# mLSTM layer of a fp32r decoder step: value projection with tokens stationary, gate columns beside the first head's values, shuffle for the sample's row pairs, and the first heads' order

## The chip, the cores and the metric

The kernel runs on one core of a Trainium2 chip. The metric is device microseconds of one execution, as the median of three runs. TensorE is called PE, VectorE DVE, ScalarE ACT, GpSimd POOL and the queue that issues the transfers SP, as the profile does.

## What is computed

One inference step of a two-layer decoder trunk on 320 tokens: one prompt of 256 and a sample group of 8 sequences with 8 tokens each. Layer 0 mixes tokens by a spatial gating MLP, layer 1 by an mLSTM matrix memory, and behind each mixer stands a gated feed-forward layer with a short convolution. The change lies in layer 1's mixer, and there in how `v` and the gates `i`, `f` are projected:

```python
p = x @ w_in                                   # x: tokens x 1024, already normed
qk_pre = p[..., :QK_B]                         # 2048 columns: 8 heads of q, 8 of k
v      = p[..., QK_B:QK_B + D_B]               # 2048 columns: 8 heads x 256
o_pre  = p[..., QK_B + D_B:QK_B + 2 * D_B]     # 2048 columns
i_pre, f_pre = the last 16 columns             # 8 input gates, 8 forget gates
...
ig = i_pre + b_i;  lf = log_sigmoid(f_pre + b_f)
h, C, n, m = mlstm_chunkwise(q, k, v, ig, lf, C0, n0, m0)   # all gates of a head from cumulated lf
```

## The kernel before, in words

Activations lie transposed (features on partitions, 320 token columns). Every fp32 operand is split in a high and a low fp32r half, and a product is three matmuls: high by high, high by low, low by high. A weight tile of 128 x 1024 numbers is brought by SP (`prefetch`, 4 raw buffers), then split by ACT (`wh`, the cast, L167) and DVE (`wl`, the difference, L168) one block ahead of its use (3 buffers of halves). `block` then issues 24 matmuls (8 slices of the features, three products) with a 128 x 128 weight slice stationary and the 320 tokens moving, into one PSUM bank of the pool `psm` (3 banks); all else takes its banks from `psa` (5).

Layer 1's mixer, `layer_b`, goes head by head (h = 0 to 7). A head's six blocks are q, k, two of v and two of o. Its steps by name:

- `gates` (L729): the gates' block `pg`, whose weights hold each gate column twice (16 matmuls); the norm's column sums, `norm_cols`, `norm_row` and `norm_twice`; then head 0's q, k, v, v, o, o and head 1's q, and between them on DVE and ACT the chain that makes the gates: a log-sigmoid (L777 to L781, with two loads of ACT tables), two scans (L782, L787), and exponentials into `Xf` and `RS`. `Xf` is spread over the partitions by a matmul into `pMb`, `RS` is turned to columns by transposes into `pt`, from where DVE makes `cols` (L819) and `gm` (L822).
- `qk_epi`: a q or k block leaves PSUM by way of `bpad`, the four taps `bcv` (one on ACT, three on DVE, L842), a tanh, `qs` and its halves.
- `v_epi` (L859): a v block leaves as `vTb` (two ACT copies). `v_nat` (L918) turns `vTb` by six transposes to tokens on partitions, `pv`, and scales and splits it to `vh`, `vl` (L928, L929).
- `scores`, `weigh`: the decay-weighted products of q and k, `psc` to `Pf` (L899) to `Ph`, `Pl`, `Ps`. `k_nat` (L931): three transposes of k into `pk`, then `kz` (L943, L944) and `kgh`, `kgl`.
- `hand_over` (`inter` into `num`, `state_sample` into four banks `pcs`), `close` (`state_out` adds `pcs` to the states `C` on DVE, L989; `numer` into `num`; `state_prompt` into `pCp`), `stats`, `scaled`, `finish` (transposes `phn`, then the rows that the output projection takes).

The sample's 64 tokens are wanted on 128 partitions, each group of 16 twice in a block of 32 (`spread`, `twice`); before, the ACT copy of `v_epi` doubles the columns, so that the transpose yields doubled rows. The order on each engine is a list schedule of the recorded order: PE's is pinned to the program's, DVE, ACT and POOL work off their queues strictly in order, and `behind(x)` keeps what it encloses behind instruction x on x's engine.

Of the kernel before, what the change touches and what calls it, by code (L numbers as in the profile page):

```python
# [38 lines left out]
class Net:  # L39
# [23 lines left out]
    def weights(self):  # L63
# [67 lines left out]
    def prefetch(self, n, m):  # L131
# [15 lines left out]
        while len(self.halved) < min(m, len(self.wq)):  # L147
# [9 lines left out]
            if self.wq[i][0] is self.I["b_wg"]:  # L157

                nc.scalar.copy(wh[:, :, 64:], raw[:, :, 64:])
                nc.scalar.copy(wl[:, :, :64], raw[:, :, :64])  # L160
                nc.vector.tensor_tensor(wl[:, :, 64:], raw[:, :, 64:], wh[:, :, 64:].bitcast(F32), op=SUB)
                self.halved.append((None, wl))
                continue
            step = 2 if i == 0 else 4 if i < 4 else kn
            for c in range(0, kn, step):
                c = slice(c, c + step)
                self.last_split = nc.scalar.copy(wh[:, c, :], raw[:, c, :])  # L167
                self.last_low = nc.vector.tensor_tensor(wl[:, c, :], raw[:, c, :], wh[:, c, :].bitcast(F32), op=SUB)  # L168
# [527 lines left out]
    def layer_b(self):  # L696
# [5 lines left out]
        with ExitStack() as ctx:  # L702
# [26 lines left out]
            def gates(rp):  # L729
# [33 lines left out]
                gr = rp.tile([64, T], F32, name="gr")  # L763
                nc.scalar.copy(gr, pg[64:, :T])
                nc.vector.tensor_tensor(gr, pg[:64, :T], gr, op=ADD)
                p0 = self.psm.tile([P, 512], F32, tag="pm", name="pm")
                (wh, wl), _ = self.take()
                self.rows(p0, wh, wl, 1, self.x_rhs, True, False)
                self.norm_cols()
                self.rows(p0, wh[:, 1:, :], wl[:, 1:, :], 7, lambda k: self.x_rhs(1 + k), False, True)  # L770
                self.norm_row()
                self.norm_twice()
                nc.vector.tensor_tensor(zi, gr[:40], self.rb[:40, :], op=MULT)
                qk_epi(0, 0, p0)
                state_in(0)
                nc.vector.tensor_scalar(zi, zi, bif[:, 0:1], None, op0=ADD)
# [24 lines left out]
                nc.vector.tensor_tensor(seg(g[:, TP:]), seg(a[:, TP:]), ML.unsqueeze(2).to_broadcast([8, NB, NS]), op=SUB)  # L801
                nc.scalar.activation(RS[32:40, 0:T], g, AF.Exp)
# [56 lines left out]
            def v_epi(h, j, ps):  # L859
                vT = lp.tile([P, 384], F32, tag="vT", name="vTb", bufs=2)  # L860
                nc.scalar.copy(vT[:, :TP], ps[:, :TP])
                nc.scalar.copy(spread(vT[:, TP:]), twice(ps[:, TP:T]))
                S[h].setdefault("vT", []).append(vT)

            def scores(h):
                s = S[h]
                q, qh, ql = s["q"]
                k, kh, kl = s["k"]
                rows = s["rows"]
                pb = s.get("spread", rows)  # L870
                sc = self.psa.tile([P, 512], F32, tag="pa", name="psc")
                mm3(sc[:, :TP], kh, kl, qh, ql, True, True)
                mm(sc[:, TP:384], k[:, P:TP], q[:, P:TP], True, True)
                mm(sc[:, 384:448], s["ks"], q[:, TP:T], True, True)
# [43 lines left out]
            def v_nat(h):  # L918
                s = S[h]
                pv = [self.psa.tile([P, 512], F32, tag="pa", name="pv") for _ in range(2)]  # L920
                dsts = [pv[t // 2][:, (t % 2) * DV:] for t in range(3)]
                for t in range(3):
                    for e in range(2):
                        self.tr(dsts[t][:, e * P:(e + 1) * P], s["vT"][e][:, t * P:(t + 1) * P], self.ident)
                for t in (2, 0, 1):
                    dst = dsts[t]
                    sc = self.rc[:, t:t + 1] if t < 2 else self.rc2
                    s["vh"] = nc.scalar.activation(vh[:, t, :DV], dst[:, :DV], AF.Copy, scale=sc)  # L928
                    s["vl"] = nc.vector.scalar_tensor_tensor(vl[:, t, :DV], dst[:, :DV], sc, vh[:, t, :DV].bitcast(F32), op0=MULT, op1=SUB)  # L929

            def k_nat(h, bank=None):  # L931
                s = S[h]
                ks = s["k"][0]
                pk = bank or self.psa.tile([P, 512], F32, tag="pa", name="pk")
                for t in range(3):
                    self.tr(pk[:, t * P:(t + 1) * P], ks[:, t * P:(t + 1) * P] if t < 2 else s["ks"], self.ident)
                kgh = hp.tile([P, 2, P], F32R, tag="kgh", name="kgh", bufs=1)
# [4 lines left out]
                for i in range(2):  # L942
                    nc.scalar.activation(kz[:, i, :], src, AF.Copy, scale=gm[:, i, h:h + 1])  # L943
                    nc.vector.scalar_tensor_tensor(kz[:, i, :], src, gm[:, 2 + i, h:h + 1], kz[:, i, :].bitcast(F32), op0=MULT, op1=ADD)  # L944
# [126 lines left out]

            with tc.tile_pool(name="rows", bufs=1) as rp:
# [3 lines left out]
            vh = hp.tile([P, 3, CW], F32R, name="vh")  # L1076
            vl = hp.tile([P, 3, CW], F32R, name="vl")
# [5 lines left out]
            nc.gpsimd.memset(vh[:, :, DV:DV + 1].bitcast(F32), 1.0)  # L1083
            nc.gpsimd.memset(vh[:, :, DV + 1:].bitcast(F32), 0.0)
            nc.gpsimd.memset(vl[:, :, DV:].bitcast(F32), 0.0)
# [31 lines left out]
            k_nat(0, self.psm.tile([P, 512], F32, tag="pm", name="pk"))  # L1117
            v_nat(0)
            with self.behind(S[0]["vl"]):
                weigh(0)  # L1120
            for h in range(1, NH):
# [9 lines left out]
                ps = blk()  # L1131
# [7 lines left out]
                ps = blk()  # L1139
# [7 lines left out]
                v_epi(h, 0, ps)  # L1147
# [5 lines left out]
                with self.behind(*S[h]["halves"]):  # L1153
                    ps = blk()
# [22 lines left out]
                if h == 1:  # L1177
                    v_nat(h)
# [46 lines left out]
    def run(self):  # L1225
        nc, tc, I, O = self.nc, self.tc, self.I, self.O
        with tc.tile_pool(name="const", bufs=1) as cp, tc.tile_pool(name="xp", bufs=1) as xp, \
# [9 lines left out]
            self.xl = xp.tile([P, KD, T], F32R, name="xl")  # L1237
            self.vecs = cp.tile([P, NVEC], F32, name="vecs")
# [33 lines left out]
def _lay_out(i):  # L1272
# [30 lines left out]
    for h in range(NH):  # L1303
        order += [h, NH + h, 16 + 2 * h, 17 + 2 * h, 32 + 2 * h, 33 + 2 * h]
    w = i["b_w_in"][0]
    a["b_win"] = _blocks(w[:, :48 * P], order)
    g = np.zeros((KD, P, P), w.dtype)
# [63 lines left out]
```

## Time and profile before

| what | value |
|---|---|
| median of three runs | 949.35 us (949.16 to 949.36) |
| the profiled execution's own time | 949.44 us |
| its span | 947.7 us |
| PE busy | 940.8 us, 99% of the span |
| DVE, ACT, POOL busy | 675.1 us, 517.7 us, 85.1 us |
| granted TensorE clock, mean | 0.999 |
| bytes moved | 156.97 MB, 166 GB/s |

The table's busy times are sums over the whole span. Rows of the timeline begin with the start and the duration in us, then engine, line, operation, output <- inputs, shape, count, and in brackets the idle time before and what ended it. Matmuls overlap, so what one costs is the distance between two starts, not its duration. Layer 1's mixer runs from about 422.8 to 712 us.

### The profile page before, as it was taken

What the parts mean: (1) busy time and instruction counts of PE and PEld (TensorE: products, weight loads), DVE (VectorE), ACT (ScalarE), POOL (GpSimd) and SP (SyncE); (2) the same over time, 40 slices, a digit from 0 to 9 for tenths busy, and PEclk for the clock granted to TensorE, in tenths of its full rate; (3) what the DMA queues carried; (4) which work ended last, traced back from release to release, by engine and by line L of the source; (5) the groups of instructions that cost most, each with busy time, mean ns of one, the idle gap of its engine ahead of it and who ended that gap; (6) DMA issues with size and microseconds to landing.
All of it is one profiled execution on the core that took longest, in us unless ns stands there. A gap on an engine that the chain in (4) does not pass through costs nothing.

```text
span 947.7 us, 17236 instructions
## 1 busy us (share of the span) xinstructions
PE 940.8 (99%) x6549; PEld 919.5 (97%) x6549; DVE 675.1 (71%) x1244; ACT 517.7 (55%) x940; POOL 85.1 (9%) x300
## 2 busy tenths in 40 slices
PE   9999999999999999999999999999999999999997
PEld 8789999999999999999999999999999999999997
DVE  6668985577777764458898987787778777775542
ACT  7557444354554444347787776575756455444332
POOL 2100000010000000003211001010011111100001
PEclk9999999999999999999999999999999999999999
DMA  8736344444444445456667555734474444445621
GB/s 288 222 126 180 128 141 144 148 153 143 149 156 151 144 148 157 147 169 224 227 204 230 191 187 198 250 124 145 161 213 145 145 157 155 139 147 153 200 85 57
DMA packets 58311, 156.97 MB, mean 166 GB/s; under 512 B 6916, under 2 KB 19852, under 8 KB 58228
## 3 DMA queue, kind: packets, MB, share of 16 engines
q1 hardware_dynamic: 58084, 155.61, 51.2%
q8 instruction: 52, 0.85, 0.4%
q14 instruction: 31, 0.25, 0.1%
q10 hardware_dynamic: 144, 0.26, 0.1%
HBM read 143.89 MB, written 11.95 MB: 164 GB/s over the span
## 4 chain that ended last, share of the span: by engine, by line
PE 99%; ACT 0%; POOLq 0%; DVE 0%; issue 0%; DVEq 0%; ACTq 0%
PE pm L48 83%; PE pv L48 5%; PE num L48 2%; PE pvs L48 2%; PE pyt L48 1%; PE pmix L48 1%; PE py L48 1%; PE psc L48 1%; PE pCp L48 1%; PE pcs L48 1%; PE pv L51 1%; PE phn L51 0%; PE pw L48 0%; PE pk L51 0%; PE pg L48 0%; PE pc L48 0%
## 5 line engine op out<-in xcount | busy, mean ns | idle before, releaser
L167 ACT CAST wh<-raw 128x1024 fp32r<-128x1024 f32 (+4 forms) x252 | 254.5, 1012 | 287.1 <-PE pm L48 154.2
L168 DVE TENSOR_TENSOR wl<-raw,wh 128x1024 fp32r<-128x1024 f32 (+4 forms) x252 | 296.0, 1178 | 117.2 <-ACT wh L167 114.4
L48 PE MATMUL pm<-xh,wh 128*128 128x320 f32 x1216 | 377.9, 311 | 0.0
L48 PE MATMUL pm<-xh,wl 128*128 128x320 f32 x1216 | 375.8, 309 | 0.0
L48 PE MATMUL pm<-xl,wh 128*128 128x320 f32 x1216 | 375.7, 309 | 0.0
L48 PEld LDWEIGHTS pm<-xh,wh 128*128 128x128 f32 x1216 | 228.3, 188 | 0.7
L48 PEld LDWEIGHTS pm<-xl,wh 128*128 128x128 f32 x1216 | 228.4, 188 | 0.0
L48 PEld LDWEIGHTS pm<-xh,wl 128*128 128x128 f32 x1216 | 228.3, 188 | 0.0
L48 PE MATMUL pm<-yh_f,wh 128*128 128x320 f32 x308 | 95.3, 309 | 0.0
L48 PE MATMUL pm<-yh_f,wl 128*128 128x320 f32 x308 | 95.0, 308 | 0.0
L48 PE MATMUL pm<-yl_f,wh 128*128 128x320 f32 x308 | 95.0, 308 | 0.0
L48 PEld LDWEIGHTS pm<-yl_f,wh 128*128 128x128 f32 x308 | 57.8, 188 | 0.0
L48 PEld LDWEIGHTS pm<-yh_f,wh 128*128 128x128 f32 x308 | 57.8, 188 | 0.0
L48 PEld LDWEIGHTS pm<-yh_f,wl 128*128 128x128 f32 x308 | 57.8, 188 | 0.0
L542 DVE SCALAR_TENSOR_TENSOR fcv<-fpad,vecs,fcv 128x336 f32<-128x336 f32 x88 | 49.5, 565 | 2.0 <-ACT fcv L540 0.6
L307 DVE TENSOR_TENSOR xT<-pm,xT 128x320 f32<-128x320 f32 x38 | 18.5, 490 | 31.4 <-PE pm L48 31.4
L48 PE MATMUL pm<-yhb,wh 128*128 128x320 f32 x128 | 40.3, 315 | 0.0
L48 PE MATMUL pm<-yh_a,wh 128*128 128x320 f32 x128 | 39.6, 309 | 0.0
L48 PE MATMUL pm<-yl_a,wh 128*128 128x320 f32 x128 | 39.5, 309 | 0.0
L48 PE MATMUL pm<-yh_a,wl 128*128 128x320 f32 x128 | 39.5, 309 | 0.0
L48 PE MATMUL pm<-yhb,wl 128*128 128x320 f32 x128 | 39.5, 309 | 0.0
L48 PE MATMUL pm<-ylb,wh 128*128 128x320 f32 x128 | 39.5, 309 | 0.0
(321 smaller groups left out, 1350.9 us busy)
## 6 DMA issues: line engine op xcount, KB each, us to landing
raw<-in_f_up SPq DMA_DIRECT2D x88, 512.0 KB, 3.5
raw<-in_b_win SPq DMA_DIRECT2D x48, 512.0 KB, 4.4
raw<-in_f_dn SPq DMA_DIRECT2D x28, 448.0 KB, 3.3
C<-in_C SPq DMA_DIRECT2D x32, 258.0 KB, 5.0
raw<-in_a_win SPq DMA_DIRECT2D x16, 512.0 KB, 3.5
raw<-in_a_wo SPq DMA_DIRECT2D x16, 512.0 KB, 3.6
out_Cs<-C SPq DMA_DIRECT2D x32, 256.0 KB, 3.8
raw<-in_f_dn SPq DMA_DIRECT2D x14, 512.0 KB, 3.5
```

The source lines that it names most:

```text
L48: self.pin(self.nc.tensor.matmul(out, lhsT, rhs, start=start, stop=stop))
L51: self.pin(self.nc.tensor.transpose(out, in_, ident))
L167: self.last_split = nc.scalar.copy(wh[:, c, :], raw[:, c, :])
L168: self.last_low = nc.vector.tensor_tensor(wl[:, c, :], raw[:, c, :], wh[:, c, :].bitcast(F32), op=SUB)
L307: self.nc.vector.tensor_tensor(x, ps[:, :T], x, op=ADD)
L542: nc.vector.scalar_tensor_tensor(cv, pd[:, i:i + NC], self.vec(w + i * KF), cv, op0=MULT, op1=ADD)
```

## The change

Seven things change together.

1. **Values with tokens stationary.** `values(h, i)` takes a 128-token slice of x (high or low half) as stationary operand and 256 value columns of the weights as moving one, into three banks `pv`, one for each group of 128 rows (two of the prompt, one of the sample). Per slice of the features that is three matmuls for each prompt group and two for the sample. `v_epi`, `v_nat`, the copies `vTb` and the six transposes go.
2. **The sample's rows in pairs.** A new tile `xs` holds for each feature slice two stationary operands: the sample's high half with its low half in the other 16 rows of each block of 32, and the high half with zeros. POOL fills it behind each norm block (two copies, eight times) and clears it once at the start. The two halves of a pair come out as separate rows of `pv`; `v_out` shuffles the rows by 16 within 32 on DVE and adds (`vx`, `vs`).
3. **Gates beside head 0's values.** Head 0's value matrix is 272 columns wide, the last 16 of them the gates, in three weight tiles of 7, 7 and 5 slices of 128. The block `pg` of 16 matmuls goes; instead DVE scales the 16 columns to `gt`, three transposes bring them to rows (the new `pg`, in the middle of head 0's q block), and three DVE operations make `zi`.
4. **Order of head 0.** The values come first (three pieces, with the norm's small matmuls between them), then q, k, o, o and head 1's q; before, v and v stood between k and o. `psc` (`products`) and `pk` (`turn`) of head 0 now stand ahead of `pMb` and `pt`.
5. **Order of head 1.** `v_out` takes its first two groups at once and the third behind `k_nat`; the splits of some weights are held behind `kz` or behind a step of the gate chain.
6. **Banks.** Head 1's three `pv` come from `psm`, from head 2 on one of three; `pk` moves to `psa` for heads 1 and 7.
7. **Memory.** `vh` and `vl` move to a pool that lives longer.

The core of the diff:

```diff
@@ weights
-        add(I["b_wg"], 0, 8)
+        for i, kn in enumerate((7, 7, 5)):
+            add(I["b_wv0"], i, kn)
...
-                add(I["b_win"], 6 * h + r, 8)
+                if r not in (2, 3):
+                    add(I["b_win"], 4 * h + (r if r < 2 else r - 2), 8)
+                elif h:
+                    add(I["b_wv"], 2 * h + r - 4, 8)
@@ residual_norm
+        if gcol == V_MIX + 8:
+            rows = self.xs[:, m, :].rearrange("p (j g d s) -> p j d g s", j=2, g=4, d=2)
+            xh, xl = [x[:, m, TP:].rearrange("p (g s) -> p g s", g=4) for x in (self.xh, self.xl)]
+            self.nc.gpsimd.tensor_copy(rows[:, :, 0], xh.unsqueeze(1).to_broadcast([P, 2, 4, 16]))
+            self.nc.gpsimd.tensor_copy(rows[:, 0, 1], xl)
@@ gates
-                pg = self.psm.tile([P, 512], F32, tag="pm", name="pg")
-                (_, wg), _ = self.take()
-                for k in range(KD):
-                    mm(pg[:, :T], wg[:, k, :], self.xh[:, k, :], k == 0, False)
-                    mm(pg[:, :T], wg[:, k, :], self.xl[:, k, :], False, k == KD - 1)
...
+                values(0, 0)
+                self.norm_cols()
+                values(0, 1)
+                self.norm_row()
+                self.norm_twice()
+                values(0, 2)
+                gt = rp.tile([P, 3, 64], F32, name="gt")
+                nc.gpsimd.memset(gt, 0.0)
+                for t in range(3):
+                    nc.vector.tensor_scalar(
+                        gt[:, t, :].rearrange("p (i e) -> p i e", e=32)[:, :, :8],
+                        S[0]["pv"][t][:, DV:DV + 16].rearrange("p (i e) -> p i e", e=8), norm(t), None, op0=MULT)
...
+                for t in range(3):
+                    self.tr(pg[:64, t * P:(t + 1) * P], gt[:, t, :], self.ident)
...
-                v_epi(0, 0, self.block(KD, self.x_rhs))
-                v_epi(0, 1, self.block(KD, self.x_rhs))
+                v_out(0)
                 o_epi(0, 0, self.block(KD, self.x_rhs))
                 o_epi(0, 1, self.block(KD, self.x_rhs))
+                self.prefetch(0, self.used + 2, [last])
                 ps = self.block(KD, self.x_rhs)
+                with self.behind(weight):
+                    self.prefetch(0, self.used + 2)
+                products(0)
+                turn(0, self.psm.tile([P, 512], F32, tag="pm", name="pk"))
@@ values and v_out
+                for k, c, first, last in ks:
+                    for t in range(2):
+                        xh, xl = self.tokens(self.xh[:, k, :], t), self.tokens(self.xl[:, k, :], t)
+                        mm(pv[t], xh, wh[:, c], first, False)
+                        mm(pv[t], xl, wh[:, c], False, False)
+                        mm(pv[t], xh, wl[:, c], False, last)
+                for k, c, first, last in ks:
+                    mm(pv[2], self.xs[:, k, :P], wh[:, c], first, False)
+                    mm(pv[2], self.xs[:, k, P:], wl[:, c], False, last)
...
+                    if t == 2:
+                        nc.vector.stream_shuffle(vx, src, [(i + 16) % 32 for i in range(32)])
+                        nc.vector.tensor_tensor(vs, vx, src, op=ADD)
+                        src = vs
@@ the loop over heads
-                ps = blk()
+                with self.behind(*([S[0]["kz"]] if h == 1 else [])):
+                    values(h, 0)
...
                 with self.behind(*S[h]["halves"]):
-                    ps = blk()
+                    values(h, 1)
                 if h == 1:
-                    with self.behind_split():
+                    v_out(1, (0, 1))
+                    with self.behind(S[1]["vl"]):
                         scaled(0)
-                v_epi(h, 1, ps)
...
-                k_nat(h, self.psm.tile([P, 512], F32, tag="pm", name="pk"))
+                k_nat(h)
...
-                if h > 1:
-                    v_nat(h)
+                v_out(h, (0, 1, 2) if h > 1 else (2,))
```

What the queues hold at two places. PE, end of the gates' stage, before: behind head 1's q block (`pm` ahead of the first row) stand the spread of the gates, their columns, head 0's scores, the turn of k, the turn of v, and then head 1's k block.

```order
L48 MATMUL pMb<-Xf,first 128x392
L51 MATMUL pt<-ident,RS 128x128 x2
L51 MATMUL pt<-ident,RS_4531 128x128
L48 MATMUL psc<-qh,kh 128x256
L48 MATMUL psc<-qhl,kh 128x256
L48 MATMUL psc<-qh,khl 128x256
L48 MATMUL psc<-qs 128x128
L48 MATMUL psc<-qs,ks 128x64
L51 MATMUL pk<-ident,qs 128x128 x2
L51 MATMUL pk<-ident,ks 128x128
L51 MATMUL pv<-ident,vTb 128x128 x6
L48 MATMUL pm<-xh,wh 128x320
```

The same place of PE in the changed kernel:

```order
L48 MATMUL psc<-qh,kh 128x256
L48 MATMUL psc<-qhl,kh 128x256
L48 MATMUL psc<-qh,khl 128x256
L48 MATMUL psc<-qs 128x128
L48 MATMUL psc<-qs,ks 128x64
L51 MATMUL pk<-ident,qs 128x128 x2
L51 MATMUL pk<-ident,ks 128x128
L48 MATMUL pMb<-Xf,first 128x392
L51 MATMUL pt<-ident,RS 128x128 x2
L51 MATMUL pt<-ident,RS_4553 128x128
L48 MATMUL pm<-xh,wh 128x320
```

Scores and the turn of k moved ahead of the gates' spread and columns, and the turn of v is gone.

DVE behind the copy of `cols` before, up to the second `kz`, which head 0's state update on PE waits for:

```order
L819 COPY cols<-pt 128x288
L880 SCALAR_TENSOR_TENSOR Qz<-qs,pMb 128x8x8
L820 TENSOR_SCALAR cols<-cols 128x3x8
L884 SCALAR_TENSOR_TENSOR w<-pMb,cols,mxb 128x64
L822 TENSOR_SCALAR gm<-cols,mk 128x8 x4
L929 SCALAR_TENSOR_TENSOR vl<-pv,rc_4632,vh 128x256
L929 SCALAR_TENSOR_TENSOR vl<-pv,rc,vh 128x256
L899 SCALAR_TENSOR_TENSOR Pf<-psc,w 128x448
L944 SCALAR_TENSOR_TENSOR kz<-pk,gm,kz 128x128
L929 SCALAR_TENSOR_TENSOR vl<-pv,rc,vh 128x256
L316 TENSOR_TENSOR Pl<-Pf,Ph 128x384
L944 SCALAR_TENSOR_TENSOR kz<-pk,gm,kz 128x128
```

DVE at the same place in the changed kernel:

```order
L833 COPY cols<-pt 128x288
L856 SCALAR_TENSOR_TENSOR bcv<-bpad_4538,vecs,bcv 128x344
L834 TENSOR_SCALAR cols<-cols 128x3x8
L940 SCALAR_TENSOR_TENSOR Qz<-qs,pMb 128x8x8
L836 TENSOR_SCALAR gm<-cols,mk 128x8 x4
L944 SCALAR_TENSOR_TENSOR w<-pMb,cols,mxb 128x64
L998 SCALAR_TENSOR_TENSOR kz<-pk,gm,kz 128x128
L856 SCALAR_TENSOR_TENSOR bcv<-bpad_4538,vecs,bcv 128x344 x2
L959 SCALAR_TENSOR_TENSOR Pf<-psc,w 128x448
L998 SCALAR_TENSOR_TENSOR kz<-pk,gm,kz 128x128
```

The three `vl` have left this stretch (they come some twenty rows earlier), three taps of head 1's q have moved into it, and the low half `Pl` has moved behind the second `kz`.

More of the change, by code (lines that the diff above doesn't have):

```diff
@@ L857, in qk_epi, with norm, values @@
                 s["qk"[j]] = (qs, hh, ll)
[L859 to L865, printed above, removed]
+            def norm(t):
+                return self.rc[:, t:t + 1] if t < 2 else self.rc2
+            def values(h, i):
+                s = S[h]
+                if h:
+                    w, k0, kn = DV, 4 * i, 4
+                else:
+                    w, k0, kn = DV + 16, 3 * i, min(3, KD - 3 * i)
+                if i == 0:
+                    pv = []
+                    for t in range(3):
+                        if h == 1 or h > 1 and t == 0:
+                            pv.append(self.psm.tile([P, 512], F32, tag="pm", name="pv")[:, :w])
+                        else:
+                            pv.append(self.psa.tile([P, 512], F32, tag="pa", name="pv")[:, :w])
+                    s["pv"] = pv
+                pv = s["pv"]
+                (wh, wl), _ = self.take()
+                wh, wl = [x.rearrange("p k c -> p (k c)") for x in (wh, wl)]
+                ks = [(k0 + k, slice(k * w, k * w + w), k0 + k == 0, k0 + k == KD - 1) for k in range(kn)]
+                for k, c, first, last in ks:
[7 more added lines that the diff above has]
+                    mm(pv[2], self.xs[:, k, P:], wl[:, c], False, last)
@@ L874, in scores @@
                 mm(sc[:, 384:448], s["ks"], q[:, TP:T], True, True)
+            def scores(h):
+                s = S[h]
+                q, rows = s["q"][0], s["rows"]
+                pb = s.get("spread", rows)
+                if h:
+                    products(h)
+                sc = s["sc"]
                 dec = rows[:, 384:392]
@@ L1138, in layer_b @@
                 state_in(h)
-                ps = blk()
+                with self.behind(*([S[0]["kz"]] if h == 1 else [])):
+                    values(h, 0)
                 if h == 1:
```

106 lines of the change are left out of this document (52 added, 54 removed).

## The prediction

> **What bounds the kernel now.** I read the page's busy times first, then its chain of the work that ended last.
>
> ```profile
> PE 940.8 (99%) x6549; PEld 919.5 (97%) x6549; DVE 675.1 (71%) x1244; ACT 517.7 (55%) x940; POOL 85.1 (9%) x300
> PE 99%; ACT 0%; POOLq 0%; DVE 0%; issue 0%; DVEq 0%; ACTq 0%
> ```
>
> PE is 99% of both, so a matmul saved is worth its whole spacing, and any other engine matters only where PE comes to wait for it. The 71% of DVE are an average. The windows by stage (columns: stretch, length, PE, weight loads, DVE, ACT, POOL, clock, DMA share, GB/s) show the end of the gates' stage, head 1's first part, and a period of two later heads.
>
> ```profile
> 438.90:453.57 14.67, 14.67 (x104) 14.34 (x103) 13.63 (x30) 11.72 (x22) 4.33 (x10) 1.00 0.54 182
> 453.57:465.00 11.43, 11.43 (x104) 10.51 (x102) 11.23 (x34) 10.66 (x29) 2.30 (x9) 1.00 0.55 195
> 479.70:507.10 27.40, 27.40 (x220) 26.48 (x216) 25.34 (x58) 22.07 (x50) 4.84 (x12) 1.00 0.66 213
> ```
>
> DVE works 13.63 of 14.67 us, then 11.23 of 11.43: around heads 0 and 1 it keeps up by tenths of a microsecond. A faster PE gets to meet DVE there. In the later heads DVE has 2.06 us spare of 27.40.
>
> **The change on PE.** Starts of matmuls with 320 and with 256 moving columns, first and last of a run:
>
> ```profile
> 519.77 0.31 PE L48 MATMUL pm<-xh,wh 128*128 128x320 f32 x1
> 523.15 0.31 PE L48 MATMUL pm<-xh,wl 128*128 128x320 f32 x1
> ```
>
> ```profile
> 937.84 0.28 PE L48 MATMUL pyt<-wh,yl_f 128*128 128x256 f32 x1
> 941.34 0.28 PE L48 MATMUL pyt<-wh,yl_f 128*128 128x256 f32 x1
> ```
>
> 23 intervals in 3.38 us are 0.1470 each, 30 in 3.50 are 0.1167. On the line between them 272 columns cost 0.1243. The turn of v that goes, and what follows it:
>
> ```profile
> 525.03 0.82 PE L51 MATMUL pv<-ident,vTb 128*128 128x128 f32 x6
> 525.60 0.40 PE L48 MATMUL pm<-xh,wh 128*128 128x320 f32 x1
> 525.84 0.31 PE L48 MATMUL pm<-xl,wh 128*128 128x320 f32 x1
> ```
>
> Six transposes take 0.57 us, 0.095 each; the first matmul behind them is 0.24 from its successor, 0.1 over the usual. Heads 1 to 7: before 48 x 0.1470 + 0.57 = 7.62, now 64 x 0.1167 = 7.47, so **-0.15 a head**, -1.05 for seven. A third more matmuls nearly eat what the narrower ones save.
>
> The Trainium skill, page "TensorE: Matmul & The Clock Gate", section "Back-to-back issue gap", speaks against this: by it the sustained spacing is set by weight load and matmul together, about 81 ns at 128 columns and 131 ns at 512. By that rule 256 columns would cost about 0.92 of 320, an estimate by a line between its figures; the trace has 0.79.
>
> Head 0 also loses the gates' block:
>
> ```profile
> 422.77 0.31 PE L48 MATMUL pg<-xh,wl 128*128 128x320 f32 x1
> 425.36 0.31 PE L48 MATMUL pm<-xh,wh 128*128 128x320 f32 x1
> ```
>
> That is 2.59 us. Before 7.06 + 0.57 + 2.59 = 10.22; now 64 x 0.1243 = 7.95, three transposes 0.29 and one restart 0.10, 8.34: **-1.88**. PE alone thus gives -2.93, and up to -0.3 more if the wait ahead of `pt` goes (below): 949.44 - 3.2 = 946.2.
>
> **Where DVE takes it back.** PE's rows around head 0's close (the first two are the norm's spread and what followed it), then DVE's and ACT's:
>
> ```profile
> 429.56 0.51 PE L48 MATMUL pb<-dg,ones 128*128 128x320 f32 x2
> 430.05 0.39 PE L48 MATMUL pm<-xh,wh 128*128 128x320 f32 x1
> 451.25 0.82 PE L48 MATMUL pMb<-Xf,first 128*128 128x392 f32 x2
> 451.91 0.49 PE L51 MATMUL pt<-ident,RS 128*128 128x128 f32 x3
> 453.89 0.39 PE L48 MATMUL pm<-xh,wh 128*128 128x320 f32 x1
> 457.58 1.08 PE L48 MATMUL num<-C,Qz 128*32 128x258 f32 x16
> 459.27 0.41 PE L48 MATMUL pm<-xh,wh 128*128 128x320 f32 x1
> 464.21 0.28 PE L48 MATMUL pCp<-vh,kgh 128*128 128x258 f32 x1
> ```
>
> ```profile
> 438.91 0.48 DVE L781 SCALAR_TENSOR_TENSOR zi<-zi,az 8x320 f32<-8x320 f32 x1 [1.22 <-ACT az L779]
> 445.96 0.41 DVE L846 SCALAR_TENSOR_TENSOR qs<-bth,bcv 128x256 f32<-128x256 f32 x1
> 446.44 0.47 DVE L788 TENSOR_TENSOR g<-g,Xf 8x320 f32<-8x320 f32 x1
> 453.57 0.45 DVE L819 COPY cols<-pt 128x288 f32<-128x288 f32 x1
> 457.62 0.34 DVE L944 SCALAR_TENSOR_TENSOR kz<-pk,gm,kz 128x128 fp32r<-128x128 f32 x1
> 462.85 0.68 DVE L989 TENSOR_TENSOR C<-C,pcs 128x512 f32<-128x512 f32 x1
> ```
>
> ```profile
> 434.81 1.28 ACT L778 ACT_TABLE_LOAD   x1
> 438.41 0.47 ACT L779 ACTIVATE az<-az 8x320 f32<-8x320 f32 x1
> ```
>
> Two `pMb` at 0.15 leave about 0.3 of the 0.66 us from 451.25 to 451.91 as a wait for `RS`. With `psc` and `pk` moved ahead, PE has other work there, so I let it go.
>
> The gate chain starts later, for the gates now come behind three pieces of values instead of first. On PE: values to 431.8 (422.77 + 7.95, 0.49 for the norm's spread and, an estimate at the transposes' 0.095, 0.6 for its six column sums), half of q's block 1.8, the transposes 0.29: 433.9. Six DVE rows (two `vl`, four short ones) bring it to about 436.0. On ACT then come 0.2 of starting, a cast of 1.0 and a tap of 0.6 that stand in its queue (the two groups below), and two table loads and two functions at 1.28 and 0.47: 441.3. So `zi`, 438.91 before, starts at 441.3, **2.4 us later**. Behind it DVE has two splits fewer than before, and a pair `qs` more (445.96 to 446.44, 0.48):
>
> ```profile
> L167 ACT CAST wh<-raw 128x1024 fp32r<-128x1024 f32 x211 | 220.6, 1047 | 233.7 <-PE pm L48 109.4 <-issue 102.9 <-PE pvs L48 11.1
> L840 ACT ACTIVATE bcv<-bpad,vecs 128x344 f32<-128x344 f32 x16 | 10.8, 673 | 2.8 <-DVE bpad L835 2.8
> L168 DVE TENSOR_TENSOR wl<-raw,wh 128x1024 fp32r<-128x1024 f32 x211 | 257.2, 1222 | 95.1 <-ACT wh L167 92.6 <-PE pm L48 1.9
> L842 DVE SCALAR_TENSOR_TENSOR bcv<-bpad,vecs,bcv 128x344 f32<-128x344 f32 x48 | 27.3, 568 | 3.1 <-ACT bcv L840 2.7
> L929 DVE SCALAR_TENSOR_TENSOR vl<-pv,rc,vh 128x256 fp32r<-128x256 f32 x24 | 11.2, 476 | 0.0
> L316 DVE TENSOR_TENSOR Pl<-Pf,Ph 128x384 fp32r<-128x384 f32 x8 | 4.4, 556 | 0.4 <-ACT Ph L315 0.4
> ```
>
> A row's successor starts some 0.08 before its end, so I count 1.14, 0.49, 0.40 and 0.48. DVE's 13.63 become 13.63 - 2 x 1.14 + 0.48 = 11.83, and with 0.5 for a cast that a split must await, `cols` starts at 441.3 + 12.3 = **453.6**, where it was. PE's k block of head 1 starts at 453.89 - 1.88 = 452.0.
>
> From `cols` to the second `kz` were 4.05 us; three `vl` (1.20) and `Pl` (0.48) leave, three taps (1.47) and about 0.35 of waiting for ACT's tap come: 4.19. The second `kz` runs from 457.8 to 458.15. PE, with k's 24 x 0.147 from 452.0, is at `num` by 455.5; `num` and `pcs` took 1.69 together before (457.58 to 459.27), the second half of `pcs` some 0.3 of it, so PE stands ahead of that half at about 457.0: **a new wait of 1.1 us**. The values of head 1 then start at 458.5, against 459.27: of 1.88 us 0.8 are left. The third add to `C`, 5.23 behind the second `kz` before, has one tap more ahead of it: 457.8 + 5.23 + 0.49 = 463.5, its end 464.2. PE, with 0.2 more for the values, reaches `pCp` at 463.65, **waits 0.5** and runs it at 464.2: level with 464.21, the lead gone. Half of head 1's -0.15 lies behind that: its second values +0.2, its transposes -0.57. With six heads at -0.15: -0.37 - 0.90 = **-1.27**. The profiled execution took 949.44, so 948.17, and 0.09 less for the median: 948.1.
>
> **What is small or hidden.** The shuffle is not in the trace. The nearest row is `vl`, 256 columns out of PSUM too, 0.40 from start to start; the shortest of 256 columns is `qs` with 0.33 (0.41 less the overlap); from above I bound it by the scan, the slowest DVE row for its size, 0.81 for 320 columns, so 0.65 for 256:
>
> ```profile
> 439.88 0.81 DVE L782 TENSOR_TENSOR_SCAN g<-rst,zi 8x320 f32<-8x320 f32 x1
> ```
>
> I take 0.40, and 0.40 for the add: 0.80 us of DVE a head, with 0.66 to 1.05 as ends. The spare 2.06 in a later period hides it, and the o blocks (3.5 us each) stand between the values and their first use. ACT gains: 32 copies of `vTb` go. The page "VectorE: DVE Perf Modes", section "The perf-mode tier table", of the Trainium skill gives the shuffle only its 1x rate, some 2400 ns for 2048 columns; that makes an estimate of 0.30 for 256, and the sum would be the same.
>
> The clearing of `xs` doubles a POOL row near the start, of 1.80 us:
>
> ```profile
> 0.80 1.80 POOL L363 MEMSET v_a<- 64x2048 f32 x1 [0.29 <-POOLq L1352]
> 4.29 0.37 POOL L300 CAST xh<-xl 128x64 fp32r<-128x64 f32 x1 [1.20 <-DVE xl L216]
> ```
>
> ```profile
> 5.44 0.41 PE L48 MATMUL pvs<-wh,xh 128*128 128x256 f32 x1
> ```
>
> POOL idles 1.20 ahead of the next cast, so that comes 0.6 later, ends at 5.3, and PE, which needs it, starts at 5.44: nothing. Without that cover it costs the 0.6. Banks and memory: three `vl` at 0.40 empty a head's three `pv` in 1.2 us, and each block behind them lasts 3.5, so one bank fewer for the blocks costs nothing while DVE is less than 2.3 us late; later than that, PE loses what goes beyond it. The DMA brings 5 slices fewer of gate weights, at a share of 0.54 to 0.66: nothing.
>
> **The rivals.** *DVE keeps pace* (0.35). One split held back less, or a table load that starts ahead of its input, lets `kz` come a microsecond sooner, and both waits vanish. For: all of it hangs on 1.6 us in a queue of 12; against: DVE had 0.2 us spare in that stretch. It gives PE's sum, 946.2.
>
> *DVE becomes the bound* (0.07, the other side). The sample's `vl` waits for shuffle and add at the end of a head's queue; if that passes the o block behind it, `pcs` waits in each head. For: 25.34 of 27.40 busy; against: the first user is one block off, and the loss starts only when more than 2.06 us a period come on top. The period of two heads gets 1.6; at the upper end, 2.1, it is over, and with each of seven heads late by the pair, 0.80, that is +5.6 in place of the -1.27: 954.9.
>
> *A spacing that does not follow the columns* (0.03). If two groups in turns, with a new stationary slice each time, kept PE to the 0.147 of 320 columns, a head's values would cost 64 x 0.147 = 9.41 in place of 7.47: 7 x 1.94 = +13.6, 961.7 (0.135, midway, gives 956.7). The 0.1167 above, where each matmul has a new stationary slice too, speaks against it. The rule of the Trainium skill on the back-to-back gap, named above, is of this kind; with its ratio it would give about 956.
>
> **How the numbers follow.** The forecast has 0.55, at 947.2 to 950.1: below if the new waits are half as long, above if `kz` and `C` each come a microsecond later. With *keeps pace* and its 0.2 for the wait ahead of `pt`, the range is 946.0 to 950.1, and 0.17 lies outside. A measurement of this kernel tells 0.2%, 1.9 us: faster is below 947.45, slower above 951.25. Faster gets the 0.35 and a twentieth of the forecast's: 0.40. Slower 0.10: the last two rivals. Same 0.50.
>
> **What would show it.** Right: values spaced by 0.117 and 0.124; `zi` near 441.3 and `cols` near 453.6; PE idle about 1.1 us ahead of the second half of `pcs`, 0.5 ahead of `pCp`; head 1's first o block level with before; a period of two later heads of 27.1. Wrong: `zi` ahead of 440.5, no wait at `kz`, a shuffle over 0.65, or a wait for the sample's `vl` in any later head.

## The result, and the profile after

The changed kernel takes **950.75 us** (median of 21 runs, 949.48 to 952.75), the kernel before 949.38 us in as many: ratio 1.0013 (95% interval 1.0007 to 1.0019). The interval lies above 1, so the kernel is slower, by less than the 0.2% that I took as the bound of a change. I had forecast 948.1 and a range up to 950.1. The profiled execution took 951.69 us, 2.25 more than that of before, with a span of 949.8.

The page's busy times and chain of the changed kernel:

```profile
PE 941.3 (99%) x6616; PEld 919.5 (97%) x6616; DVE 680.4 (72%) x1271; ACT 510.7 (54%) x906; POOL 98.9 (10%) x318
PE 97%; DVE 1%; ACT 1%; issue 1%; POOL 0%; POOLq 0%; DVEq 0%; ACTq 0%
```

PE is still nearly all of the chain, but 1% each has gone to DVE, ACT and issue: there are now places where PE waits. The list of PE's waits from the gates on names them (in total, times, longest), and the windows around the longer one show what followed:

```profile
PE pcs L48 <- DVE Pf L959: 1.2, 1, 1.2
PE pb L48 <- DVE dg L279: 0.2, 1, 0.2
```

```profile
455.90:459.30 3.40, 2.23 (x33) 1.32 (x32) 3.12 (x11) 3.13 (x9) 1.34 (x4) 1.00 0.88 337
459.30:459.90 0.60, 0.60 (x9) 0.59 (x6) 0.60 (x1) 0.60 (x3) 0.60 (x1) 1.00 0.09 33
459.90:463.40 3.50, 3.50 (x19) 3.50 (x18) 3.50 (x10) 3.50 (x10) 1.31 (x3) 0.51 0.36 72
463.40:466.70 3.30, 3.30 (x30) 3.30 (x29) 3.30 (x8) 2.99 (x7) 1.11 (x4) 1.00 1.00 363
```

The column before the DMA share is the granted clock. After a stretch in which PE worked 2.23 of 3.40 us, it stands at **0.51 for 3.5 us**, with PE busy all the while: 19 matmuls where the next 3.3 us hold 30. PE's rows there, the first value matmuls of head 1 among them, and a later head's 64, first row and the row behind the last:

```profile
456.92 0.53 PE L48 MATMUL pcs<-vh,kz 32*128 32x256 f32 x3
458.62 0.38 PE L48 MATMUL pcs<-vh,kz 32*128 32x256 f32 x1 [1.17 <-DVE Pf L959]
459.32 0.39 PE L48 MATMUL pv<-wh,xh 128*128 128x256 f32 x1
460.25 0.42 PE L48 MATMUL pv<-wh,xh 128*128 128x256 f32 x1
460.46 0.41 PE L48 MATMUL pv<-wh,xl 128*128 128x256 f32 x1
```

```profile
490.37 0.28 PE L48 MATMUL pv<-wh,xh 128*128 128x256 f32 x1
498.05 0.28 PE L48 MATMUL psc<-qh,kh 128*128 128x256 f32 x1
```

At the lower clock the spacing is 0.21; at the full one 64 matmuls take 7.68 us, **0.1200** each. Start of the same work in the two profiled executions, from PE's rows:

| work | before | after | difference |
|---|---|---|---|
| head 1's k block | 453.89 | 452.21 | -1.68 |
| `num` of head 0 | 457.58 | 455.91 | -1.67 |
| head 1's first values | 459.27 | 459.32 | +0.05 |
| `pCp` of head 0 | 464.21 | 466.05 | +1.84 |
| `num` of head 1 | 477.97 | 479.47 | +1.50 |
| `num` of head 7 | 668.08 | 669.67 | +1.59 |
| `pb`, the next norm's spread | 711.77 | 713.65 | +1.88 |
| end of the span | 947.7 | 949.8 | +2.1 |

Head 0 gains 1.68 of the 1.88 forecast; the wait at `pcs` takes all of it; in this execution the lower clock takes most of as much again; six later heads give nothing.

### The profile page after: what moved, and what is told of

It is laid out like the page before. It is cut to its first block, busy times and chain, and to the rows that moved or that the text cites. A ratio compares the mean times of both kernels' runs of the same rounds, so it can differ in the third digit from the quotient of the medians.

```text
span 949.8 us, 17382 instructions
## 1 busy us (share of the span) xinstructions
PE 941.3 (99%) x6616; PEld 919.5 (97%) x6616; DVE 680.4 (72%) x1271; ACT 510.7 (54%) x906; POOL 98.9 (10%) x318
## 4 chain that ended last, share of the span: by engine, by line
PE 97%; DVE 1%; ACT 1%; issue 1%; POOL 0%; POOLq 0%; DVEq 0%; ACTq 0%
PE pm L48 75%; PE pv L48 11%; PE num L48 2%; PE pvs L48 2%; PE pyt L48 1%; PE pmix L48 1%; PE py L48 1%; PE pCp L48 1%; PE pcs L48 1%; PE psc L48 1%; PE phn L51 0%; PE pw L48 0%; ACT wh L164 0%; DVE wl L166 0%; PE pc L48 0%
## 5 line engine op out<-in xcount | busy, mean ns | idle before, releaser
L48 PE MATMUL pm<-xh,wh 128*128 128x320 f32 x1088 | 338.5, 311 | 0.0
L48 PE MATMUL pm<-xl,wh 128*128 128x320 f32 x1088 | 336.4, 309 | 0.0
L48 PE MATMUL pm<-xh,wl 128*128 128x320 f32 x1088 | 336.3, 309 | 0.0
L48 PEld LDWEIGHTS pm<-xl,wh 128*128 128x128 f32 x1088 | 204.4, 188 | 0.0
L48 PEld LDWEIGHTS pm<-xh,wl 128*128 128x128 f32 x1088 | 204.3, 188 | 0.0
L48 PE MATMUL pv<-wh,xh 128*128 128x256 f32 (+2 forms) x196 | 62.8, 324 | 0.0
L48 PE MATMUL pv<-wl,xh 128*128 128x256 f32 (+2 forms) x196 | 62.4, 322 | 0.0
L48 PE MATMUL pv<-wh,xl 128*128 128x256 f32 (+2 forms) x196 | 62.4, 322 | 0.0
L48 PEld LDWEIGHTS pv<-wh,xh 128*128 128x128 f32 x196 | 38.0, 196 | 3.2 <-ACT wh L164 0.3
L48 PEld LDWEIGHTS pv<-wl,xh 128*128 128x128 f32 x196 | 38.0, 196 | 2.9 <-DVE wl L166 0.5
```

Of the source, the lines that this page charges most:

```text
L48: self.pin(self.nc.tensor.matmul(out, lhsT, rhs, start=start, stop=stop))
```

## The experiments

Theory A: DVE, ACT and POOL do not finish head 0's `Pf` and `kz` sooner than before, so PE waits; the idling halves PE's clock for a window; and value matmuls cost 0.1200, not 0.1167. Rivals: the slow stretch is contention of the new matmuls for operands; the shuffle costs PE time.

**The same kernel once more** (no edit).

> The changed kernel itself once more, on the chip of its neighbours and beside the same runs of the kernel before, so that the other kernels can be set against it. Median 950.2 to 951.3; about half of the executions with a mean clock of 0.996 to 0.998, those some 1.6 us longer than the ones at 0.999.

Median 950.13, ratio 1.0005 (0.9996 to 1.0013). Of these 11 executions one had a mean clock of 0.997 (951.7); of the 21 before, 7 had 0.996 or 0.997 (median 951.69) and 14 had 0.998 or 0.999 (950.26). An execution with the lower clock is thus 1.4 us longer, and how often the clock falls varies: a third, then a tenth, where I had written half. The profiled execution of this run waited as long and kept its clock; below the windows stand its first value matmul of head 1 and its `pCp`:

```profile
455.90:459.30 3.40, 2.22 (x27) 1.24 (x26) 3.11 (x12) 2.67 (x7) 1.24 (x3) 1.00 0.92 368
459.30:462.70 3.40, 3.40 (x37) 3.27 (x34) 3.40 (x10) 3.40 (x10) 1.59 (x3) 1.00 0.37 104
```

```profile
459.78 0.38 PE L48 MATMUL pv<-wh,xh 128*128 128x256 f32 x1
465.24 0.39 PE L48 MATMUL pCp<-vh,kgh 128*128 128x258 f32 x1
```

The same matmuls, behind the same wait, are spaced 0.1200 here: they are not slow by themselves. From the first values to `pCp` are 5.46 us, against 6.73 at the lower clock and 4.94 before; 0.2 of the 5.46 are a gap just ahead of `pCp`.

**PE kept busy through the wait.**

```diff
+                if h == 0:
+                    for _ in range(13):
+                        mm(s["pcs"][0][:, :DV], self.xh[:, 0, :P], self.xh[:, 1, :DV], True, True)
```

> The changed kernel with 13 extra matmuls of 256 columns (1.5 us) into the first pcs bank of head 0 ahead of the real ones, which then overwrite it: PE works through the time in which it stood idle, and the wait for Pf itself stays as it is. Theory A (the idle stretch is what lets the clock be halved): granted clock 1.00 from 459 to 463 in the profile, mean clocks of 0.998 or 0.999 as of the kernel before in every execution, the spread of the times shrinks, and the median is that of the executions without a lower clock, 949.6 to 950.2. Rival B (the slow stretch comes from the new matmuls and their operands, not from the idling): half of the executions still show 0.996 to 0.998, median 950.75 up to 951.1.

```profile
456.87 1.81 PE L48 MATMUL pcs<-xh 128*128 128x256 f32 x13
458.62 0.39 PE L48 MATMUL pcs<-vh,kz 32*128 32x256 f32 x4
459.29 0.39 PE L48 MATMUL pv<-wh,xh 128*128 128x256 f32 x1
```

```profile
459.30:462.70 3.40, 3.40 (x32) 3.40 (x29) 3.40 (x9) 3.40 (x11) 1.26 (x2) 1.00 0.59 146
```

The real work starts at the same 459.29, but no execution of 11 has a clock below 0.998 (0.998 to 1.000). Median 950.36, a little over the range of A, for DVE's order behind it came out otherwise (a wait of 0.3 for `vl` is new). This count alone does not decide, since the unedited kernel on the same chip (the run above) lost its clock in only one of 11. Against contention stands that run's profile, with the same matmuls at 0.1200. For the idling stand the runs with more of it: the two that follow and the one with the banks freed sooner show a lower clock in 14 of 15 executions.

**A filler in the wrong bank.**

```diff
+                            if (h, i, g) == (0, 0, 3) and v is vh:
+                                for _ in range(14):
+                                    mm(s["pk"][:, 384:], self.xh[:, 0, :P], self.xh[:, 1, :P], True, True)
```

> The changed kernel with 14 extra matmuls of 128 columns on PE (into an unused part of the bank pk) ahead of the fourth pcs matmul of head 0, where PE stood idle for 1.17 us at 457.4 to 458.6; the wait itself stays. The output is unchanged. Theory A (the idle stretch is what halves the granted clock, 0.51 over the next 3.5 us, and that costs about 1.6 us in the executions in which it happens): matmuls of head 1's first values spaced 0.120 again in place of 0.21, granted clock 1.00 there, no execution below 0.999 of mean clock, the median 0.8 to 1.6 us lower than the changed kernel's 950.75, so 949.2 to 950.0. Rival B (the 0.21 spacing is contention of the new matmuls with DVE, ACT and the DMA for operands, and the clock record only follows it): spacing stays near 0.21 for those matmuls, median 950.75 or later by up to 0.3.

It told something else: the extra matmuls themselves waited 4.2 us for `kgl`, which still read that bank. Median 957.71 (ratio 1.0088, 1.0074 to 1.0102). Behind the longer idling all four executions show a lower clock (0.994 and 0.995), the profiled one for two windows:

```profile
457.50:461.50 4.00, 0.06 (x1) 0.00 (x0) 3.81 (x10) 3.75 (x10) 2.28 (x5) 1.00 0.49 160
461.50:464.80 3.30, 3.02 (x14) 3.02 (x14) 3.00 (x9) 3.30 (x10) 0.05 (x1) 0.52 0.67 184
464.80:468.20 3.40, 3.40 (x25) 3.06 (x25) 2.69 (x5) 1.43 (x6) 1.23 (x5) 0.50 0.00 0
```

**The wait itself, first try**: head 1's three taps and head 0's `Ph`, `Pl` behind `kz`.

```diff
-                qk_epi(h, 0, ps)
+                qk_epi(h, 0, ps, *([S[0]["kz"]] if h == 1 else []))
...
-            with self.behind(S[0]["vl"]):
+            with self.behind(S[0]["vl"], S[0]["kz"], S[0]["kzc"]):
                 weigh(0)
```

> The changed kernel with head 1's three DVE taps, and head 0's low halves Pl, held behind the second kz of head 0, so that the gate columns gm, the weights w, Pf and kz come earlier. Theory A (the wait of PE at pcs is DVE's and ACT's queue behind cols, and the lower clock follows the wait): the wait falls from 1.17 to 0.2 to 0.5 us, the clock stays at 1.00, median 1.5 to 2.4 us below the changed kernel's 950.75: 948.4 to 949.3. Rival B (the slow matmuls are contention in head 1's first values whatever PE waits for): only the 0.7 to 1.0 of the wait comes back, 949.8 to 950.1, and the spacing of 0.21 stays. Rival C (the taps held back are wanted soon after, and the wait moves to head 1's later steps): within 0.3 of 950.75.

Median 953.26 (ratio 1.0037, 1.0024 to 1.0051): the wait moves on, as rival C has it, but the time is 2.2 us above its range. PE waited 0.93 and 0.28 for `kz` and then 1.42 for `kgl`, whose bank head 1's second group takes; four of five executions show 0.995 to 0.997.

**Five edits at the same place**: the taps and `weigh` as above, `Qz` behind `gm`, `kz` in two tiles, and head 1's first values group by group.

```diff
+                order = [(t, k) for t in range(2) for k in ks] if (h, i) == (1, 0) else [(t, k) for k in ks for t in range(2)]
+                for t, (k, c, first, last) in order:
```

> The changed kernel with five edits around head 0's close: head 1's taps behind kz, head 0's Ph and Pl behind kz, Qz behind gm, kz in two tiles, and head 1's first values group by group, so that the second bank is wanted 1.1 us later. Theory A: gm at 454.5 instead of 455.4, Pf ahead of 457.6, PE idle ahead of pcs 0.3 to 0.6 us instead of 1.17, no wait for kgl at the values, clock 1.00: 948.6 to 949.4. Rival C (what is held back is wanted at once, and the wait moves to the values' bank or to C): 950.0 to 952. Rival B (contention): 949.8 to 950.2 with the spacing of 0.21.

The wait at `pcs` is gone, the values start at 458.07, and the microsecond is lost two steps on:

```profile
460.68 0.39 PE L48 MATMUL pv<-wh,xh 128*128 128x256 f32 x1 [0.92 <-DVE kgl L1005]
462.90 0.36 PE L48 MATMUL pv<-wh,xs 128*128 128x256 f32 x1 [0.53 <-DVE bpad L849]
```

Median 950.50 (1.0012, 1.0003 to 1.0021): rival C. The clocks are 0.998 and 0.999, in spite of the wait of 0.92.

**The banks freed sooner**: with these edits, k's block leaves PSUM ahead of `C`, and `kgh`, `kgl` stand ahead of the taps and casts.

```diff
+                    inter(0)
+                    state_sample(0)
+                    tail = qk_epi(h, 1, ps, later=True)
+                    for g in (0, 1):
+                        state_out(0, g)
```

> The edits of the run with five edits, and the banks of head 1's values freed sooner: head 1's k block leaves PSUM ahead of the first C adds, kgh and kgl stand ahead of the taps, of Ph and Pl and of the next casts. Theory (what is left of the change's gain hangs on DVE's and ACT's order between cols and C): head 1's values start at 458.1 and run through without the waits of 0.9 and 0.5, pCp at 463.5 to 464.3 against 464.2 of the kernel before, median 949.0 to 949.8. Rival (DVE has that much to do there whatever the order, and the wait moves to pCp, which needs the third C add): pCp at 465, 950.0 to 950.8.

Median 955.69 (1.0061, 1.0048 to 1.0073), far above both ranges: DVE stood 2.83 us in its queue behind a row of head 1 that waited for a transfer, PE waited 3.01 us for `C`, and `pCp` came at 469.41. All six executions show a lower clock, 0.994 to 0.997.

**That row and k's taps held behind `C`**:

```diff
+                    with self.behind(S[0]["cadd"]):
+                        tail()
```

> The edits of the second run around head 0's close, with two more: head 1's decay column w, for which DVE stood 2.8 us behind a transfer there, and head 1's k taps are held behind the last add to C. Theory (the rest of the change's gain hangs on this stretch of DVE's and ACT's order): values of head 1 from 458.1 with less than 0.4 us of waits, pCp at 463.6 to 464.4, clock 1.00, median 948.9 to 949.9, that is within 0.1% of the kernel before. Rival (the stretch holds as much work as time, and a wait comes back at C, at the weights of the second values or at head 1's scores): 950.0 to 952.

Now the values run through from 458.02, and PE waits for the add to `C`:

```profile
464.95 0.39 PE L48 MATMUL pCp<-vh,kgh 128*128 128x258 f32 x1 [1.21 <-DVE C L1048]
```

Median 951.31 (1.0019, 1.0010 to 1.0028): the rival. The clocks are 0.998 and 0.999, in spite of the wait of 1.21.

**The same with less for DVE to do**: this kernel leaves out the three DVE taps of head 1's q, and holds head 1's `Qz` behind `C`.

```diff
-                        for i in (1, 2, 3):
+                        for i in (1, 2, 3) if (h, j) != (1, 0) else ():
```

> The kernel of the run before with 1.5 us less work for DVE in the same stretch: head 1's q gets only the first of its four taps (that part of the computation is left out), and head 1's Qz is held behind C as its w is. Theory (between cols and the adds to C, DVE and ACT have more work than PE leaves them time, so that the order only moves the wait about): the wait of 1.2 us ahead of pCp shrinks to 0.3 or less, pCp at 463.5 to 464.0 in place of 464.95, the median 1.0 to 1.5 us below the 951.31 of that kernel: 949.8 to 950.3. Rival (the wait hangs on ACT's or a transfer's order, DVE's work is not it): pCp still near 464.9, median within 0.4 of 951.3.

```profile
463.13 0.39 PE L48 MATMUL pCp<-vh,kgh 128*128 128x258 f32 x1
```

The wait is gone, and the median is 949.27, 2.0 below (I had said 1.0 to 1.5): with 1.5 us of DVE work less, and `Qz` moved, `pCp` comes 1.8 us sooner. So DVE's queue between `cols` and the adds to `C` lies on PE's path: each order tried that serves `kz` sooner serves a bank or `C` later. It is not DVE's work alone, for in the run before DVE itself stood 0.90 us waiting for ACT's scaling of `kz` and 0.70 for ACT's `kgh`. I found no order that does all the work and beats the kernel before; that there is none is not shown.

**The order of `psc` and `pk` undone.**

```diff
-                products(0)
-                turn(0, self.psm.tile([P, 512], F32, tag="pm", name="pk"))
                 pb = self.psa.tile([P, 512], F32, tag="pa", name="pMb")
...
+                products(0)
+                turn(0, self.psm.tile([P, 512], F32, tag="pm", name="pk"))
```

> One part of the change undone: psc and pk of head 0 stand behind pMb and pt again, as before. PE then has no work while it waits for Xf and RS (about 1 us more there), and comes to pcs later by as much, where it had 1.17 us to wait anyway. Theory A: the wait at pcs shrinks to 0.2 to 0.5, head 1's values start within 0.3 us of the changed kernel's 459.3, and no halved clock, or a rarer one, follows: 949.5 to 950.3. Rival O (the order gives PE a whole microsecond that is not lost later): 951.5 to 952.

Median 950.65 (1.0013, 1.0005 to 1.0022), between the two ranges and nearer to A; clocks 0.998 and 0.999. PE now waits at `pMb` and no longer at `pcs`, and head 1's values start at 459.30:

```profile
451.44 0.93 PE L48 MATMUL pMb<-Xf,first 128*128 128x392 f32 x2 [0.95 <-ACT Xf L806]
```

(There is a wait of 1.1 us for `kgl` behind it.) The new order saves PE a microsecond that it then spends waiting.

**Without shuffle and add.**

```diff
-                    if t == 2:
-                        nc.vector.stream_shuffle(vx, src, [(i + 16) % 32 for i in range(32)])
-                        nc.vector.tensor_tensor(vs, vx, src, op=ADD)
-                        src = vs
```

> The changed kernel without the shuffle and the add that join the sample's pairs of rows (the sample's values are then incomplete, so part of the computation is left out). The prediction held that their 0.8 us of DVE a head is hidden: then the spacing and head period stay and the median is within 0.5 us of 950.75. Rival (the pair is late in each head and PE pays for it): 0.4 to 0.9 us a head less in seven heads, 945 to 948.

Median 950.85 (1.0013, 1.0004 to 1.0022), 0.1 from the changed kernel: the pair is hidden. Five of these ten executions show a clock of 0.997.

**Why 0.1200.** q's halves as stationary operand in heads 2 to 7:

```diff
+                        if h > 1:
+                            xh, xl = [self.tokens(x, t) for x in s["q"][1:]]
```

> The changed kernel in which from head 2 on the prompt's value matmuls take q's halves as stationary operand in place of the slices of x (the values are then not those of the reference: part of the computation is replaced). In the changed kernel they are spaced 0.1200 us, where the last stage's matmuls of the same shape, and the scores of the same stage, have 0.1167. Theory S (the operand x, a slice of a wider tile, makes the weight load slower): 0.1167 here. Rival M (the moving side, weights that come from the split buffers, or the stage's traffic makes the difference): 0.1200 stays. By S the 288 matmuls concerned would save 0.96 us in all, by M nothing.

Of the six groups without a wait, four showed 0.118, between the two, and two 0.1135, below both (the sample's, unchanged, 0.120); the 958.05 us hold waits for q. Then one variation a head:

```diff
+                    pv = [x[:, 512 - w:] if h == 2 else x[:, :w] for x in pv]
...
+                order = [(t, k) for t in range(2) for k in ks] if h == 4 else [(t, k) for k in ks for t in range(2)]
...
+                    if h == 5:
+                        xh, xl = [self.tokens(y, t) for y in Y[2 * h - 4]]
+                    if h == 6:
+                        a, b = self.xh[:, 0, :DV], self.xl[:, 0, :DV]
+                    if h == 7:
+                        xh, xl, a, b = a[:, :P], b[:, :P], self.xh[:, k, :DV], self.xl[:, k, :DV]
+                    steps = [(xh, a), (xl, a), (xh, b)] if h != 3 else [(xh, a), (xh, b), (xl, a)]
```

> Why the value matmuls are spaced 0.1200 us and not the 0.1167 on which the prediction rested: one kernel, one variation a head, read from the spacing in each (heads 5 to 7 replace part of the computation, their values are not the reference's). Head 2: the banks' upper columns in place of the lower (theory: the place in PSUM; 0.1167 there if so). Head 3: the order xh wh, xh wl, xl wh (theory: which operand changes; other than 0.1200 if so). Head 4: all of one group of tokens, then the next (theory: the change of bank every third matmul; 0.1167 if so). Head 5: stationary slices of an earlier head's output y (theory: the place of x in SBUF; 0.1167 or at least the 0.118 seen with q). Head 6: x as the moving side too (theory: reading weights from their split buffers; 0.1167 if so). Head 7: weights stationary and x moving, 256 columns, the arrangement of the kernel before (theory: x against x; 0.1200 if x on either side does it, 0.1167 if it is x as stationary alone). Whatever shows 0.1200 excludes its theory; no time is claimed for the whole.

Spacing of the prompt's matmuls: heads 2, 3, 4, 6 and 7 0.1200 (one group of head 3 0.1196), head 5 0.1183 and 0.1174. The place in PSUM, the order of operands, the change of bank and the weights are out. With x on either side it is 0.1200, with y as stationary 0.117 to 0.118, with q 0.1135 or 0.118. What makes these differences of 2 to 6 ns stays open.

## Why the prediction was wrong, step by step

- **Right.** `zi` forecast at 441.3 stood at 441.17, `cols` at 453.85 for 453.6, head 1's k block at 452.2 for 452.0. The shuffle took 0.45 for 0.40, and it is hidden (its row, eight heads in all):

```profile
L913 DVE STREAM_SHUFFLE vx_b<-pv 128x256 f32<-128x256 f32 x8 | 3.6, 450 | 0.0
```

That head 0's gain meets DVE's queue, and that little is left of it, was the forecast's mechanism.
- **Misread, without harm: the period.** The prediction takes the 27.40 us for a period of two heads. They are one: `num` of head 2 and of head 3 stand 27.42 apart before (505.39 and 532.81) and 27.47 after, with one shuffle between them. The windows from `num` to `num`, before and after:

```profile
505.39:532.81 27.42, 27.42 (x216) 26.50 (x215) 23.95 (x56) 20.89 (x50) 3.45 (x12) 1.00 0.64 206
506.91:534.38 27.47, 27.47 (x226) 26.55 (x226) 24.85 (x58) 19.98 (x45) 4.71 (x12) 1.00 0.61 205
```

DVE gets 0.90 more, one pair, and not 1.6, and 2.6 us stay free. The rival *DVE becomes the bound* was further from its condition than its sum says, and the sign "a period of two later heads of 27.1" should have been 27.25 for one head; it measured 27.47.
- **Right in kind, too short: the wait at `pcs`.** Forecast: 1.1 us for the second `kz`, values at 458.5. Measured: 1.17 us, ahead of the fourth `pcs` matmul and not of the ninth, for `Pf`, and values at 459.32, 0.8 later. DVE's rows of the changed kernel:

```profile
453.85 0.45 DVE L833 COPY cols<-pt 128x288 f32<-128x288 f32 x1
454.73 0.58 DVE L856 SCALAR_TENSOR_TENSOR bcv<-bpad,vecs,bcv 128x344 f32<-128x344 f32 x1 [0.44 <-ACT bcv L854]
455.44 0.63 DVE L836 TENSOR_SCALAR gm<-cols,mk 128x8 f32<-128x8 f32 x4
457.94 0.62 DVE L959 SCALAR_TENSOR_TENSOR Pf<-psc,w 128x448 f32<-128x448 f32 x1 [0.18 <-POOL w L950]
458.49 0.34 DVE L998 SCALAR_TENSOR_TENSOR kz<-pk,gm,kz 128x128 fp32r<-128x128 f32 x1
```

I had added up DVE's rows from `cols` to `kz`, 4.19; it took 4.64. The path leaves DVE: `gm` waits behind a tap, ACT's exponentials behind `kz`'s scaling, which needs `gm`, and POOL's mask behind these; `Pf` can start only then. The fourth `pcs` takes the bank that `Pf` reads.
- **Failed: a wait priced at its length.** "A new wait of 1.1 us" and "waits 0.5" cost just that in the sum. The clock was no term. In the profiled execution the first values took 5.41 us (459.32 to 464.73) for 32 x 0.1200 = 3.84: 1.57 more. The forecast's 0.5 at `pCp` did not come as a wait there, for PE was later than `C`; with the clock kept it came as 0.2, so that from the values to `pCp` the clock cost 6.73 - 5.46 = 1.27 net. In the median of 21 runs it is some 0.5 (950.75 against the 950.26 of the executions that kept it). Those too lie above the range, which ended at 950.1, so the clock is not the whole of the miss.
- **Failed: 64 x 0.1167 = 7.47, "-0.15 a head".** The term is 64 x 0.1200 = 7.68 against 7.62 before, and from `num` of head 1 to that of head 7 the difference moved from +1.50 to +1.59: +0.015 a head. For six heads that is 1.0 us, the largest term of the miss wherever the clock is kept. The row I took the spacing from was of the last stage, with other operands. In the changed mixer's own stage `num`, with 258 columns, stood at 0.120 in the trace of before, but `psc`, with 256, at 0.117: neither shape nor stage alone gives it. Head 0's matmuls of 272 columns stood at 0.126 for 0.124, 0.1 us of the 0.2 that its gain fell short.
- **Not foreseen, small**: 0.3 us up to the next norm's spread, where `pb` waits 0.2 (the list of waits above).
- Sum of the profiled executions: 2.25 measured less -1.27 forecast is 3.52. Of it 1.84 stand at `pCp`, which was forecast level: 1.27 the clock and 0.57 the longer wait and the values behind it. 1.0 are the later heads, 0.3 the norm; 0.4 lie behind the last matmul, in part outside the span (2.25 against the last matmul's 1.86), and are not explained. Of the median's miss, 950.75 less 948.1 or 2.65, the clock is only some 0.5.

The Trainium skill, page "TensorE: Matmul & The Clock Gate", section "Part 1: The HAM clock gate (the "warmup" mystery)", bears on the failed step: it says that the gate passes half of the pulses after an idle window of about 3.4 us, in windows that run on by themselves. The trace agrees with the half (0.51) and the length (3.5 us), and a clock that falls in some executions only fits a window that falls as it may; it differs in the condition, for PE stood idle only 1.17 us here. That length is not the whole condition: behind waits of 0.92 to 1.21 us between matmuls of the full 128 x 128 (five edits, order undone, k's taps behind `C`) none of 33 executions shows a lower clock, though on that chip the unedited kernel lost its own in one of 11 only. Here the wait stands among the 32-column and 32-row matmuls of `num` and `pcs`, and from the first of these to the values are 3.41 us (455.91 to 459.32), where the kernel before has 1.69. Whether these matmuls count as idling was not tried. The spacing rule of the Trainium skill that stood as a rival did not come true: 0.1200 to 0.1470 is 0.82, and its 0.92 would have cost 8 us.

## What to carry to other kernels

A microsecond taken from the engine that bounds is gained only where the others deliver sooner too: follow the next thing that it needs through every engine on its way, here DVE, ACT and POOL, and not along one queue. A wait of PE costs its length and can cost, in some executions, a window at half the clock (1.4 us here); others of the same length did not, so read the granted clock behind each wait. Take a matmul's spacing from rows with the same operands, or leave it a range: 3 ns times 64 matmuls are 0.2 us a head, more than the 0.15 that each later head was to gain.

## What the runs showed of the hardware

- The granted clock fell to 0.51 for one window of 3.5 us behind a stretch with 1.17 us of idle PE, in 7 of 21 and in 1 of 11 executions of one kernel by their mean clocks. Behind 4.2 us it fell to 0.50 to 0.52 for two windows, and all four executions have a lower mean. Behind waits of 0.92 to 1.21 us between full-size matmuls none of 33 has one. The kernel runs on a single core.
- A shuffle of 128 x 256 numbers out of PSUM took 0.45 us on DVE, the add behind it 0.41.
- 256 moving columns of fp32r were spaced 0.1135 to 0.1200 us with different operands, with weight loads of 0.19 to 0.20.
